# A hybrid decoder step: RWKV's 64-row products alternate between the two halves of the partitions

## The chip, the core and the metric

The kernel runs on one core of a Trainium2 chip. The core has a matrix engine (TensorE, PE in the rows; its weight loads are PEld), VectorE (DVE), ScalarE (ACT), GpSimd (POOL) and SyncE (SP), which work on their own queues, each in order, and wait for each other by semaphores. [...] The metric is the device time of one execution in microseconds (us), the median of the runs.

## The reference

One layer of a decoder for two groups of requests that share weights: a prompt of 2048 tokens, and 8 samples of 8 tokens with caches. A token has 1024 values.

```
sh1, sc1, gt1, sh2, sc2, gt2 = ada_modulation(c)
proj = (rms_norm(x) * (1 + sc1) + sh1) @ w_in          # 1024 -> 1536 (attention) + 1792 (RWKV)
att  = three dilated windows (128,1) (512,4) (2048,16), combined by their log-sums
Pm   = P + (P_prev - P) * mu                            # RWKV: token shift
w    = -softplus(-(w0 + tanh(wl) @ w2)) - 0.5           # low rank, 64 -> 512
a    = sigmoid(a0 + al @ a2)                            # low rank, 64 -> 512
S_t  = S * decay + (S @ -kk) (kk*a)^T + v k^T ;  o = S r # 8 heads of 64 x 64, token by token
x    = x + gt1 * (concat(att, rwkv_output(o)) @ w_out)
x    = x + gt2 * (relu(h2 @ w_ff1)^2 @ w_ff2)           # 1024 -> 4096 -> 1024
```

All inputs and outputs are float32.

## The kernel before, in words

**Tiling and stages.** The prompt is cut into four windows of 512 tokens. A table (ORDER) names the stages and the times at which they are planned: i0 to i3 (norm and input projection), r0 to r3 (RWKV), a0 to a3 (attention), s (the samples' RWKV and attention), and m, p, f (mixing, output projection, MLP). A stage gets a priority that rises with its planned time, and the framework's planner then puts every engine's instructions into one fixed order: it walks through a model of the machine and takes, engine by engine, the ready instruction that comes first by priority. So the large products of the i, p and f stages (PSUM tiles named mmps, written in `mm3`, lines 320 to 322, three products per block since a float32 is split into two parts) stand between the small steps of r, a and s.

**RWKV in groups.** A window of RWKV is four groups of 128 tokens, 16 groups in all, and the samples are one more of 64. A group is two chunks of 64 tokens. Channels lie on partitions: the tile `[128, 4, W]` holds 8 heads of 64 channels as 4 pairs (hp), the even head of a pair on partitions 0 to 63, the odd one on 64 to 127 (par 0 and 1). A product over one head contracts over 64 partitions, so it uses one half of the rows of TensorE's array.

**Three such families are touched.**

- lps, in `rw_elem` (lines 553 to 563): the low-rank products. `wa2` has w2 on partitions 0 to 63 and a2 on 64 to 127; the input is `sg` (named sgl in the rows) for the first and `lm` for the second. Four products for one, into a PSUM tile of one bank, and an addition by VectorE (xx, line 563); then four for the other and its addition.
- btps, in `rw_mats` (lines 639 to 645): bk is transposed, 2 chunks x 4 pairs for par 0 into one bank, copied out by ScalarE (bkT, line 645), then the same for par 1.
- aps, in `rw_mats` (lines 653 to 663): for each chunk, after four transpositions of the values (vtps, line 649, copied to UV by ScalarE, line 650), four products bk x F for par 1 into one bank, three masked copies by VectorE (AT, AT, F; lines 660, 661, 663), then the same for par 0.

**Banks.** These tiles have the tag "e", for which there are two banks; vtps, ssps and bops take the same two, and part of attention's and the samples' tiles too. A tile gets a bank when one is free in the planner's walk.

**What follows.** AT goes through DRAM to `rw_solve` (triangular inverses), then `rw_chunk` carries the state through the two chunks, and `rw_out` normalizes and gates. The next group's `rw_elem` is issued ahead of the chunks of this one.

Of the kernel before, what the change touches and what calls it, by code (L numbers as in the profile page):

```python
# [9 lines left out]
F32 = mybir.dt.float32  # L10
F32R = mybir.dt.float32r
BF16 = mybir.dt.bfloat16
AF = mybir.ActivationFunctionType
# [109 lines left out]
class Step:  # L123
# [407 lines left out]
    def rw_elem(self, V, psv, g):  # L531
        nc = self.nc
        S = g < 0
        W, seg, nch = (64, 8, 1) if S else (128, 64, 2)
# [10 lines left out]
        lm = V.tile([128, 2, W], F32, name="lm", tag="lm")  # L545
        self.rw_mix(V, g, 12, 2, "rawl", lm)
        sg = V.tile([128, 2, W], F32, name="sgl", tag="sgl")
# [2 lines left out]
        nc.vector.tensor_scalar(sg[0:64, 0], sg[0:64, 0], 2.0, -1.0, op0=ALU.mult, op1=ALU.add)  # L550
        r["gl"] = sg[:, 1]
        xx = V.tile([128, 2, 4, W], F32, name="xx", tag="xx")
        for i, (lo, src, bias) in enumerate(((0, sg, self.w0), (64, lm, self.a0))):
            pt = psv.tile([128, 4, W], F32, name="lps", tag="e")
            for hp in range(4):
                nc.tensor.matmul(
                    pt[:, hp],
                    self.wa2[lo:lo + 64, hp * 128:(hp + 1) * 128],
                    src[lo:lo + 64, 0],
                    start=True,  # L560
                    stop=True,
                )
            nc.vector.tensor_tensor(xx[:, i], pt, bias[:, :, None].to_broadcast([128, 4, W]), op=ALU.add)
        xt = V.tile([128, 2, 4, W], F32, name="xt2", tag="xx")
        f4 = lambda t: t.rearrange("p a h t -> p (a h t)")
# [14 lines left out]
        pt = psv.tile([128, 4, W], F32, name="ssps", tag="e")  # L580
# [18 lines left out]
        F = V.tile([128, 4, nch, 128], F32, name="F", tag="F")  # L599
        bk = V.tile([128, 4, nch, 128], F32, name="bk", tag="bk")  # L600
# [29 lines left out]
    def rw_mats(self, V, psv, r, nch, masks):  # L630
        nc = self.nc
        F, bk = r["F"], r["bk"]
        F1 = V.tile([128, 4, nch, 128], F32, name="F1", tag="F1")
        nc.sync.dma_start(F1[0:64], F[64:128])
        UV = V.tile([128, nch, 8, 64], F32, name="UV", tag="UV") if "UV" not in r else r["UV"]
        r["UV"] = UV
        bkT = V.tile([128, nch, 8, 64], F32, name="bkT", tag="bkT")
        AT = V.tile([128, nch * 8, 64], F32, name="AT", tag="AT")
        for par in range(2):
            o = 64 * par  # L640
            pt = psv.tile([128, nch, 4, 64], F32, name="btps", tag="e")
            for c in range(nch):
                for hp in range(4):
                    nc.tensor.transpose(pt[:, c, hp], bk[o:o + 64, hp, c], self.ident[o:o + 64, o:o + 64])
            nc.scalar.activation(bkT[:, :, 4 * par:4 * par + 4], pt, AF.Copy)
        for c in range(nch):
            pt = psv.tile([128, 4, 128], F32, name="vtps", tag="e")
            for hp in range(4):
                nc.tensor.transpose(pt[0:64, hp], r["mv"][:, hp, 64 * c:64 * c + 64], self.ident)
            nc.scalar.activation(  # L650
                UV[64:128, c].rearrange("p h e -> p (h e)"), pt[0:64].rearrange("p h e -> p (h e)"), AF.Copy
            )
            for par in (1, 0):
                o = 64 * par
                pt = psv.tile([128, 4, 128], F32, name="aps", tag="e")
                for hp in range(4):
                    nc.tensor.matmul(pt[:, hp], bk[o:o + 64, hp, c], F[o:o + 64, hp, c], start=True, stop=True)  # L657
                u = (c * 2 + par) * 4
                mb = lambda lo, a, n: masks[lo:lo + 64, None, a:a + n].to_broadcast([64, 4, n])
                nc.vector.tensor_tensor(AT[64:128, u:u + 4], pt[0:64, :, 0:64], mb(0, 0, 64), op=ALU.mult)  # L660
                nc.vector.tensor_tensor(AT[0:64, u:u + 4], pt[0:64, :, 64:128], mb(0, 64, 64), op=ALU.mult)
                dst = (F1 if par else F)[64:128, :, c]
                nc.vector.tensor_tensor(dst, pt[64:128], mb(64, 0, 128), op=ALU.mult)
        r.update(F1=F1, bkT=bkT, AT=AT, AO=AT[0:64])
        if BO == 0:
            self.rw_bonus(V, psv, r)
# [14 lines left out]
    def rw_solve(self, V, psv, r, nch):  # L681

        nc = self.nc
        AT = r["AT"]
        nu = nch * 8
# [3 lines left out]
        for b in range(2):  # L689
            for h in range(2):  # L690
                o = 32 * b + 16 * h
                nc.sync.dma_start(dA[:, b, h].rearrange("u s t -> s u t"), AT[64 + o:80 + o, :, o:o + 16])
        dT = self.dr.tile([nu, 2, 2, 16, 16], F32, name="dT", tag="dT", bufs=3)
# [29 lines left out]
        for b in range(2):  # L723
            lo, hi, o = 64 + 32 * b, 80 + 32 * b, 32 * b
            nc.sync.dma_start(AT[hi:hi + 16, :, o + 16:o + 32], dT[:, b, 1].rearrange("u j i -> j u i"))
            nc.sync.dma_start(AT[lo:hi, :, o:o + 16], dT[:, b, 0].rearrange("u j i -> j u i"))
# [971 lines left out]
```

## Time and profile before

| | |
|---|---|
| median of 3 runs | 3586.67 us (3585.26 to 3594.71) |
| profiled execution | 3593.78 us, its span 3591.7 us |
| TensorE busy | 3317.7 us, 92% of the span, 26546 matmul records |
| weight loads | 2800.1 us, 78% |
| VectorE, ScalarE, GpSimd | 62%, 48%, 29% |

The span is the time from the first to the last instruction of the profiled execution. Busy times come from that one execution. TensorE's products overlap: one starts while the one before still drains, so the distance between starts, not the duration, says what a product costs. [...]

### The profile page before, as it was taken

To read this page: it belongs to the slowest core of one execution; us is meant where nothing else is said; L and a number is where in the kernel's file an instruction comes from. 1 tells how busy PE (TensorE), PEld (TensorE's weight loads), DVE (VectorE), ACT (ScalarE), POOL (GpSimd) and SP (SyncE) were. 2 spreads that over 40 slices of the span, in tenths; PEclk is the share of its full clock that TensorE was granted. 3 is DMA by queue.
4 is the path that set the end of the run, shared out by engine and by line. 5 is a ranking of instruction groups with operands and counts; after the bars stand their busy time and mean duration, and the time that the engine had idled before them with its cause. 6 is when DMAs were issued, how large, how long until landed. Compare 5 with 4: busy or idle time off the path is not lost. (4 is left out here: it accounts for less than half of the span.)

```text
span 3591.7 us, 67893 instructions
## 1 busy us (share of the span) xinstructions
PE 3317.7 (92%) x26546; PEld 2800.1 (78%) x26546; DVE 2241.2 (62%) x4821; ACT 1711.8 (48%) x3156; POOL 1055.9 (29%) x775
## 2 busy tenths in 40 slices
PE   6999999888979999999899999898999999789998
PEld 4886888877968777778877776686777778789998
DVE  3465555635777566778756555454666778655665
ACT  4444353545455555445555432354555445453453
POOL 2322232212233212224321122132112223354464
PEclk7999999989989999899999999999999999899999
DMA  6446644435344542325454234996542325365464
GB/s 231 141 140 172 201 133 134 124 83 101 87 131 131 130 114 83 83 80 169 138 150 124 81 84 131 262 275 212 139 118 87 89 76 166 95 193 153 148 187 153
DMA packets 731769, 496.64 MB, mean 138 GB/s; under 512 B 126134, under 2 KB 682344, under 8 KB 731448
## 3 DMA queue, kind: packets, MB, share of 16 engines
q1 hardware_dynamic: 718824, 479.65, 46.4%
q0 software_dynamic: 12624, 12.65, 1.4%
q8 instruction: 209, 3.42, 0.4%
q14 instruction: 112, 0.92, 0.1%
HBM read 424.11 MB, written 63.77 MB: 136 GB/s over the span
## 5 line engine op out<-in xcount | busy, mean ns | idle before, releaser
L262 POOL TENSOR_TENSOR wl<-stg,wh 128x640 fp32r<-128x640 f32 (+1 forms) x384 | 686.8, 1790 | 1437.7 <-ACT wh L258 1189.7
L258 ACT ACTIVATE wh<-stg 128x1024 fp32r<-128x1024 f32 x384 | 406.2, 1058 | 621.3 <-PE mmps L321 377.7
L320 PE MATMUL mmps<-h2hi,wh 128*128 128x256 f32 (+2 forms) x1864 | 625.0, 336 | 7.9 <-ACT h2hi L306 4.4
L322 PE MATMUL mmps<-h2hi,wl 128*128 128x256 f32 (+2 forms) x1864 | 625.1, 336 | 7.3 <-POOL wl L262 6.9
L321 PE MATMUL mmps<-h2lo,wh 128*128 128x256 f32 (+2 forms) x1864 | 624.8, 335 | 2.9 <-POOL h2lo L308 2.9
L262 DVE TENSOR_TENSOR wl<-stg,wh 128x384 fp32r<-128x384 f32 (+1 forms) x384 | 305.9, 798 | 295.5 <-ACT wh L258 277.8
L321 PE MATMUL mmps<-hid,wh 128*128 128x512 f32 (+2 forms) x1280 | 464.6, 363 | 9.0 <-DVE hid L1429 9.0
L320 PE MATMUL mmps<-hid,wh 128*128 128x512 f32 (+2 forms) x1280 | 465.0, 364 | 2.3 <-ACT wh L258 1.6
L322 PE MATMUL mmps<-hid,wl 128*128 128x512 f32 (+2 forms) x1280 | 464.5, 364 | 1.0 <-POOL wl L262 1.0
L320 PEld LDWEIGHTS mmps<-h2hi,wh 128*128 128x128 f32 x1864 | 357.2, 192 | 38.9 <-ACT h2hi L306 5.3
L322 PEld LDWEIGHTS mmps<-h2hi,wl 128*128 128x128 f32 x1864 | 356.9, 192 | 37.0 <-POOL wl L262 9.5
L321 PEld LDWEIGHTS mmps<-h2lo,wh 128*128 128x128 f32 x1864 | 357.3, 192 | 30.1 <-POOL h2lo L308 3.8
L262 POOL TENSOR_TENSOR wlo<-stg,whi 128x640 fp32r<-128x640 f32 x104 | 182.4, 1768 | 499.5 <-ACT whi L258 461.1
L321 PEld LDWEIGHTS mmps<-hid,wh 128*128 128x128 f32 x1280 | 245.5, 192 | 41.2 <-DVE hid L1429 11.9
L322 PEld LDWEIGHTS mmps<-hid,wl 128*128 128x128 f32 x1280 | 245.8, 192 | 35.0 <-issue 5.8
L320 PEld LDWEIGHTS mmps<-hid,wh 128*128 128x128 f32 x1280 | 245.9, 192 | 33.4 <-ACT wh L258 1.8
L1307 DVE SCALAR_TENSOR_TENSOR acc<-mmps,ada,acc 128x512 f32<-128x512 f32 (+1 forms) x280 | 179.1, 640 | 139.4 <-PE mmps L322 138.2
L320 PE MATMUL mmps<-hhi,whi 128*128 128x512 f32 (+2 forms) x608 | 218.8, 362 | 19.0 <-ACT pev L398 12.3
L320 PE MATMUL mmps<-whi,hhi 128*128 128x256 f32 (+1 forms) x816 | 234.2, 287 | 1.6 <-ACT qev L428 1.6
L321 PE MATMUL mmps<-wlo,hhi 128*128 128x256 f32 (+1 forms) x816 | 234.1, 287 | 0.0
L322 PE MATMUL mmps<-whi,hlo 128*128 128x256 f32 (+1 forms) x816 | 234.0, 287 | 0.0
L321 PE MATMUL mmps<-hlo,whi 128*128 128x512 f32 (+2 forms) x608 | 219.3, 361 | 6.6 <-POOL hlo L308 6.6
(350 smaller groups left out, 6525.9 us busy)
## 6 DMA issues: line engine op xcount, KB each, us to landing
stg<-in_w_ff_dram SPq DMA_DIRECT2D x320, 512.0 KB, 4.2
stg<-in_w_in_dram SPq DMA_DIRECT2D x104, 512.0 KB, 4.7
stg<-in_w_out_dram SPq DMA_DIRECT2D x64, 512.0 KB, 4.6
kst<-in_cache_k_dram SPq DMA_DIRECT2D x80, 256.0 KB, 5.5
vst<-in_cache_v_dram SPq DMA_DIRECT2D x80, 256.0 KB, 5.3
xt<-in_x_prompt_dram SPq DMA_DIRECT2D x32, 512.0 KB, 4.3
wada<-in_w_ada_dram SPq DMA_DIRECT2D x32, 512.0 KB, 3.7
Pd<-pev SPq DMA_DIRECT2D x56, 256.0 KB, 2.8
```

The source lines that it names most:

```text
L258: nc.scalar.activation(hi, src, AF.Copy)
L262: eng.tensor_tensor(lo[:, k], src[:, k], hi[:, k].bitcast(F32), op=ALU.subtract)
L320: nc.tensor.matmul(out, wh(k), xh(k), start=k == 0, stop=False)
L321: nc.tensor.matmul(out, wh(k), xl(k), start=False, stop=False)
L322: nc.tensor.matmul(out, wl(k), xh(k), start=False, stop=k == nk - 1)
L1307: nc.vector.scalar_tensor_tensor(o, pt[:, 0:np_], gt[:, ob, 0:1], o, op0=ALU.mult, op1=ALU.add)
```

## The change

In all three families the two halves' tiles are now made together, and the products alternate between them, one of the lower and one of the upper half of the partitions; the readers (additions, copies, masks) follow after both. For aps the pair starts with par 1 as before, and the reading order is par 1, then par 0.

```diff
-        for i, (lo, src, bias) in enumerate(((0, sg, self.w0), (64, lm, self.a0))):
-            pt = psv.tile([128, 4, W], F32, name="lps", tag="e")
-            for hp in range(4):
+        pts = [psv.tile([128, 4, W], F32, name="lps", tag="e") for _ in range(2)]
+        for hp in range(4):
+            for lo, src, pt in ((0, sg, pts[0]), (64, lm, pts[1])):
                 nc.tensor.matmul(
                     pt[:, hp],
                     self.wa2[lo:lo + 64, hp * 128:(hp + 1) * 128],
...
+        for i, (pt, bias) in enumerate(zip(pts, (self.w0, self.a0))):
             nc.vector.tensor_tensor(xx[:, i], pt, bias[:, :, None].to_broadcast([128, 4, W]), op=ALU.add)
...
+        pts = [psv.tile([128, nch, 4, 64], F32, name="btps", tag="e") for _ in range(2)]
+        for c in range(nch):
+            for hp in range(4):
+                for par in range(2):
+                    o = 64 * par
+                    nc.tensor.transpose(pts[par][:, c, hp], bk[o:o + 64, hp, c], self.ident[o:o + 64, o:o + 64])
         for par in range(2):
-            o = 64 * par
-            pt = psv.tile([128, nch, 4, 64], F32, name="btps", tag="e")
-            for c in range(nch):
-                for hp in range(4):
-                    nc.tensor.transpose(pt[:, c, hp], bk[o:o + 64, hp, c], self.ident[o:o + 64, o:o + 64])
-            nc.scalar.activation(bkT[:, :, 4 * par:4 * par + 4], pt, AF.Copy)
+            nc.scalar.activation(bkT[:, :, 4 * par:4 * par + 4], pts[par], AF.Copy)
...
+            pts = [psv.tile([128, 4, 128], F32, name="aps", tag="e") for _ in range(2)]
+            for hp in range(4):
+                for par in (1, 0):
+                    o = 64 * par
+                    nc.tensor.matmul(pts[par][:, hp], bk[o:o + 64, hp, c], F[o:o + 64, hp, c], start=True, stop=True)
             for par in (1, 0):
-                o = 64 * par
-                pt = psv.tile([128, 4, 128], F32, name="aps", tag="e")
-                for hp in range(4):
-                    nc.tensor.matmul(pt[:, hp], bk[o:o + 64, hp, c], F[o:o + 64, hp, c], start=True, stop=True)
+                pt = pts[par]
```

The planner then orders anew. On TensorE, in the first group's `rw_elem` (lps is the low-rank tile, sgl and lm the two inputs, mmps a block of the projection), the piece of the difference is:

```order
 L321 MATMUL mmps<-hlo,whi 128x512
 L322 MATMUL mmps<-hhi,wlo 128x512
-L556 MATMUL lps<-sgl,wa_1682 128x128 x4
-L556 MATMUL lps<-lm,wa_1682 128x128 x4
+L556 MATMUL lps<-sgl,wa_1682 128x128
+L556 MATMUL lps<-lm,wa_1682 128x128
+L556 MATMUL lps<-sgl,wa_1682 128x128
+L556 MATMUL lps<-lm,wa_1682 128x128
+L556 MATMUL lps<-sgl,wa_1682 128x128
+L556 MATMUL lps<-lm,wa_1682 128x128
+L556 MATMUL lps<-sgl,wa_1682 128x128
+L556 MATMUL lps<-lm,wa_1682 128x128
```

Four and four have become one and one, at the same place among the projection's blocks. All 16 groups of the prompt look so, and their transpositions (btps) too.

On TensorE, in the first group's second chunk, with the tiles' numbers (aps_1882 is par 1 and aps_1890 par 0, vtps the values' transpositions), before:

```order
L649 MATMUL vtps_1876<-ident_90,mv_1809 64x128 x4
L321 MATMUL mmps_1027<-wlo_1015,hhi_249 128x256
L322 MATMUL mmps_1027<-whi_1016,hlo_250 128x256
L320 MATMUL mmps_1027<-whi_1016,hhi_249 128x256
L321 MATMUL mmps_1027<-wlo_1015,hhi_249 128x256
L322 MATMUL mmps_1027<-whi_1016,hlo_250 128x256
L320 MATMUL mmps_1092<-whi_1016,hhi_249 128x256
L321 MATMUL mmps_1092<-wlo_1015,hhi_249 128x256
L657 MATMUL aps_1882<-F_1787,bk_1788 128x128 x4
L657 MATMUL aps_1890<-F_1787,bk_1788 128x128 x4
```

The same place now (aps_1883 is par 1, aps_1882 par 0):

```order
L651 MATMUL vtps_1876<-ident_90,mv_1809 64x128 x4
L321 MATMUL mmps_1027<-wlo_1015,hhi_249 128x256
L322 MATMUL mmps_1027<-whi_1016,hlo_250 128x256
L320 MATMUL mmps_1027<-whi_1016,hhi_249 128x256
L321 MATMUL mmps_1027<-wlo_1015,hhi_249 128x256
L322 MATMUL mmps_1027<-whi_1016,hlo_250 128x256
L320 MATMUL mmps_1092<-whi_1016,hhi_249 128x256
L321 MATMUL mmps_1092<-wlo_1015,hhi_249 128x256
L659 MATMUL aps_1883<-F_1787,bk_1788 128x128 x3
L659 MATMUL aps_1882<-F_1787,bk_1788 128x128 x3
L659 MATMUL aps_1883<-F_1787,bk_1788 128x128
L659 MATMUL aps_1882<-F_1787,bk_1788 128x128
```

Three, three, one and one stand where four and four stood: the second bank was ready in the planner's walk only when three of par 1 were placed. In most chunks the two halves of aps still stand apart, four of one and, after a stretch of mmps, four of the other.

## Rows read from the trace of the kernel before

**Rows 1.** The page's first part: busy us, share of the span, instructions.

```profile
PE 3317.7 (92%) x26546; PEld 2800.1 (78%) x26546; DVE 2241.2 (62%) x4821; ACT 1711.8 (48%) x3156; POOL 1055.9 (29%) x775
```

**Rows 2.** Busy time by stretch, last RWKV window; the columns stand ahead.

```profile
core 0: us, PE busy (x) PEld busy (x) DVE busy (x) ACT busy (x) POOL busy (x), PEclk, DMA share, GB/s
...
2756.00:3060.00 304.00, 289.24 (x2338) 231.15 (x2338) 245.54 (x470) 156.52 (x290) 91.99 (x87) 0.99 0.38 109
```

**Rows 3.** TensorE's groups by line: shapes, count, busy us, mean ns, idle before, releasers.

```profile
L657 PE MATMUL aps<-F,bk 64*128 64x128 f32 x528 | 83.3, 302 | 1.2 <-ACT UV L650 1.1
...
L556 PE MATMUL lps<-sgl,wa 64*128 64x128 f32 (+1 forms) x136 | 21.2, 301 | 11.3 <-DVE sgl L550 10.5 <-DVE sol L714 0.7
...
L644 PE MATMUL btps<-ident,bk 64*128 64x64 f32 x264 | 18.9, 237 | 8.0 <-DVE bk L620 6.6 <-DVE bk L619 1.4
```

**Rows 4.** Timeline, TensorE, first lps block: start us, us, instruction, count.

```profile
128.85 0.82 PE L556 MATMUL lps<-sgl,wa 64*128 64x128 f32 x5
129.40 0.37 PE L556 MATMUL lps<-lm,wa 64*128 64x128 f32 x1
129.51 0.27 PE L556 MATMUL lps<-sgl,wa 64*128 64x128 f32 x1
129.62 0.27 PE L556 MATMUL lps<-lm,wa 64*128 64x128 f32 x1
129.62 0.27 PE L556 MATMUL lps<-sgl,wa 64*128 64x128 f32 x1
129.73 0.27 PE L556 MATMUL lps<-lm,wa 64*128 64x128 f32 x1
129.73 0.27 PE L556 MATMUL lps<-sgl,wa 64*128 64x128 f32 x1
129.84 0.72 PE L556 MATMUL lps<-lm,wa 64*128 64x128 f32 x5
130.49 0.50 PE L320 MATMUL mmps<-hhi,whi 128*128 128x512 f32 x1
```

**Rows 5.** Timeline, TensorE: aps runs of one, four, and four and four.

```profile
242.50 0.49 PE L657 MATMUL aps<-F,bk 64*128 64x128 f32 x2
242.91 0.64 PE L225 MATMUL mps<-wada,cT 128*32 128x256 f32 x8
...
865.63 1.16 PE L657 MATMUL aps<-F,bk 64*128 64x128 f32 x8
866.72 0.38 PE L320 MATMUL mmps<-hhi,whi 128*128 128x256 f32 x1
...
377.97 1.71 PE L657 MATMUL aps<-F,bk 64*128 64x128 f32 x16
379.61 0.38 PE L322 MATMUL mmps<-whi,hlo 128*128 128x256 f32 x1
```

**Rows 6.** Timeline, TensorE: a whole btps block, and a broken one.

```profile
153.26 0.98 PE L644 MATMUL btps<-ident,bk 64*128 64x64 f32 x16
154.18 0.39 PE L322 MATMUL mmps<-whi,hlo 128*128 128x256 f32 x1
...
3016.44 0.71 PE L644 MATMUL btps<-ident,bk 64*128 64x64 f32 x9
3017.08 0.33 PE L1477 MATMUL trps<-ident,acc 128*128 128x128 f32 x1
```

**Rows 7.** TensorE's waits: waiting line, releaser, us in total, times, longest us.

```profile
PE lps L556 <- DVE sgl L550: 10.5, 5, 5.6
...
PE btps L644 <- DVE bk L620: 6.6, 4, 3.4
...
PE btps L644 <- DVE bk L619: 1.4, 2, 1.1
...
PE aps L657 <- ACT UV L650: 1.1, 1, 1.1
```

**Rows 8.** The copies out of btps: count, least, median and most ns.

```profile
L645 ACT ACTIVATE bkT<-btps x34: 365/593/599, 154.9 to 3021.6; 128x512 f32<-128x512 f32 x32, 128x256 f32<-128x256 f32 x2
```

## The prediction

> **What bounds the kernel now.** I read the page's busy shares first, then the stretches of the RWKV windows, then the three groups of products that the change touches, their rows in order of time, and last what they wait for. TensorE is busy 92% of the span, no other engine is near that [rows 1], and in the last RWKV window (2756 to 3060 us) it is busy 289 of 304 us at a granted clock of 0.99 [rows 2]. Its queue is in order, and the planner lays the projection's and the MLP's products (mmps) between the steps of RWKV. So I first ask how much TensorE time the change takes out, and then how much of that the rest can follow.
>
> The touched groups are 528 records for the matrices (aps), 136 for each half of the low rank (lps) and 264 for the transpositions (btps) [rows 3]. An fp32 product leaves two records, a transposition one: 33 chunks x 8 products x 2 = 528, 17 groups x 4 x 2 = 136, 16 x 16 + 8 = 264.
>
> **How two halves run already.** [Rows 4] is a whole lps block. Five records of sgl (partitions 0 to 63) start 0.11 us apart; at 129.40 the first of lm (64 to 127) starts although three of sgl are still to come; then one of each starts at 129.62, and again at 129.73, each half keeping its 0.11 us. So halves with banks of their own do run side by side at full pace, and the order of before already uses this where they meet, for about 3 of 8 records. The block takes 128.85 to 130.49, 1.64 us. The price of a single half is in [rows 5]: four aps products (8 records), 865.63 to 866.72, 1.09 us; one alone, 242.50 to 242.91, 0.41 us, so about 0.41 + 0.23 (n-1) us for n products: some 0.2 us of a run is spent once, whatever its length. Four and four of the same chunk in a row take 377.97 to 379.61, 1.64 us, as in lps.
>
> **Part by part.** No instruction is added or removed; on each engine the same ones stand in another order.
>
> lps: in the new order 16 of 17 blocks alternate product by product. If both halves keep the pace of [rows 4], a block costs what one half costs, 1.09 us: 16 x (1.64 - 1.09) = 8.8 us. The sample's block keeps four, filler, four.
>
> btps: 16 blocks alternate. Before, a block takes 153.26 to 154.18, 0.92 us; nine transpositions, eight of them of one half, take 3016.44 to 3017.08, 0.64 us [rows 6]. 16 x 0.28 = 4.5 us.
>
> aps: here the order does only part of what the code says. The two banks are seldom free at the same moment (one has held vtps, the other the last btps or aps), and the planner takes what is ready. Counted in the order: before, 29 runs of one product, 9 of two, 13 of three and 25 of four, all of one half, 7 of four and four, and 4 shorter mixed ones (an estimated 4.6 us in all from the same pitches). At 0.41, 0.64, 0.86, 1.09 and 1.64 us that is 11.9 + 5.8 + 11.2 + 27.3 + 11.5 + 4.6 = 72.3 us. Now 19, 14, 6 and 22 one-sided runs, 4 of four and four, 4 of the form three, three, one, one (estimated 1.3 us: half the overlap), and 9 that alternate wholly or nearly so, which I price at their longer half, 7.5 us: 7.8 + 9.0 + 5.2 + 24.0 + 6.6 + 5.2 + 7.5 = 65.3 us. It gives 7.0 us, half of it from fewer and longer runs, not from alternating. If the planner's order gave nothing, 0; if all 33 chunks alternated, 33 x 1.09 = 36 us would be left, but the order shows that they don't.
>
> Sum on TensorE: 8.8 + 4.5 + 7.0 = 20.3 us.
>
> What it does not shorten is RWKV's own chain. The first half of a block ends no sooner than before, and its readers still come one after the other: two copies of bkT of 0.593 us each [rows 8] finish about when they did, because the second had to wait for ScalarE's first and not for TensorE. The same holds for the two additions after lps and the masks after aps. So the time comes back only where TensorE would otherwise go on at once with filler and the next RWKV step is ready when it comes sooner. TensorE stood waiting at lps for sgl 5 times, at btps for bk 4 + 2 times, out of 17 blocks each [rows 7]: at about a third of the blocks the chain is late already, and there what was saved before them becomes a longer wait. I take two thirds: 20.3 x 2/3 = 13.5 us. The bounds of this share are 0 and 1.
>
> The profiled execution is 3593.8 us (3591.7 of span and 2.1 around it), 7.1 above the median of the runs, 3586.7. From its own time the sum gives 3580.3, from the median **3573.2 us**.
>
> The added wait: both banks must be free before the second product of a pair. Behind it in TensorE's queue stands whatever the planner put there, mostly mmps. Nothing of before prices it exactly: aps waited for the copy out of vtps (UV) once, 1.1 us [rows 7], the lower bound is 0 since the planner puts filler ahead of the second bank (last pair of order rows), and the upper bound a copy of 0.593 us at each of 17 + 17 + 33 = 67 places, 40 us. I take 0, nearest to the one wait seen, and keep the other end as a rival.
>
> **The rivals.**
> Not passed on (the filler is done sooner, then TensorE waits for VectorE and ScalarE): for it, the unshortened chain; against it, 289 of 304 us busy. Gain 0 to 6.8 us, a share under a third: about 3583 us.
>
> More than forecast: halves that did not overlap before, as if the pairs of starts in [rows 4] were only drawn so. Then the blocks of 1.64 and 0.92 us hold 16 records one behind the other, alternating takes half of each, and 16 x 0.82 + 16 x 0.46 + 7.0 = 27.5 us come free, two thirds of it 18 us: 3568 us. Against it: eight records of one half take 1.09 us by themselves and cost 0.11 us more each, so 16 in strict order would be 1.09 + 8 x 0.11 = 1.97 us and not the 1.64 of the rows. [...]
>
> Slower: the second bank. If the bank is still held on the chip by a reader that the planner thought done, TensorE stands still with the filler behind it. At 0.593 us for all 67 places the loss is 40 us, net of 13.5 about 26 us: 3613 us. It decides from 13.5 / 67 = 0.20 us per place. For it: the planner's costs are not the chip's, and a pair needs two free banks where one did. Against it: such waits are nearly absent before.
>
> The alternation that doesn't happen: true for most aps already by the order and in the sum; without any aps gain 13.3 x 2/3 = 8.9 us, 3577.8, inside the forecast's own range.
>
> **How the numbers follow.** A difference under 0.3% (10.8 us: 3575.9 to 3597.4) can't be told from none here. Forecast 0.60, with shares of one third to one: 3566 to 3580 us, two thirds of it below 3575.9. Not passed on 0.20, nearly all of it no change. No overlap before 0.08, faster. Second bank 0.12, slower. Faster: 0.39 + 0.08 = 0.47. Same: 0.21 + 0.18 = 0.39. Slower: 0.12 + 0.02 = 0.14. The range for 8 in 10 reaches from the full 27.5 us, 3559, to the upper part of no change, 3596, where some moved filler or a few waits for a bank still fit.
>
> **What would show it.** Right: lps blocks of about 1.1 us with sgl and lm starting in pairs, btps blocks of about 0.64 us, aps runs of 1.09 us still one-sided in most chunks, and TensorE's idle time at lps, btps and ssps up by 5 to 10 us. Wrong: blocks that stay at 1.6 us (two halves don't run together product by product), TensorE waits of half a microsecond at lps or aps for xx, bkT or UV (the second bank), or a granted clock in the last window below the 0.99 of [rows 2] because TensorE stands still more often.

## The result, and the profile after

| | before | after |
|---|---|---|
| median (7 runs each) | 3586.67 us (3582.4 to 3594.71) | 3608.16 us (3600.33 to 3616.86) |
| profiled execution, span | 3593.78, 3591.7 us | 3615.23, 3613.5 us |
| mean granted clock | 0.964 | 0.959 |
| TensorE busy, idle within the span | 3317.7, 274.1 us | 3323.0, 290.5 us |
| time at half clock | 259.9 us | 295.0 us |

The changed kernel is slower: ratio 1.0054, 95% interval 1.0036 to 1.0072. The forecast was 3573.2 us, 0.4% faster, and the time lies above the range. TensorE's idle time is the span less the busy time; the granted clock (PEclk) is, as the profile gives it, a share of full speed. In slices of 0.2 us both traces show 1.0 or 0.5, and a mean between them only where a slice holds a step from one to the other; the time at half clock is the sum of the stretches at 0.5.

The page's first part after, against [rows 1]:

```profile
PE 3323.0 (92%) x26546; PEld 2797.6 (77%) x26546; DVE 2240.5 (62%) x4821; ACT 1712.5 (47%) x3156; POOL 1055.1 (29%) x775
```

TensorE is busier by 5.3 us and idler by 16.4 us, although the blocks became shorter. That they did, the first lps block shows, against [rows 4] (timeline of TensorE; start us, us, instruction):

```profile
125.38 0.40 PE L322 MATMUL mmps<-hhi,wlo 128*128 128x512 f32 x1
125.71 0.37 PE L556 MATMUL lps<-sgl,wa 64*128 64x128 f32 x1
125.72 0.37 PE L556 MATMUL lps<-lm,wa 64*128 64x128 f32 x1
125.92 0.27 PE L556 MATMUL lps<-sgl,wa 64*128 64x128 f32 x1
125.93 0.27 PE L556 MATMUL lps<-lm,wa 64*128 64x128 f32 x1
126.03 0.27 PE L556 MATMUL lps<-sgl,wa 64*128 64x128 f32 x1
126.04 0.27 PE L556 MATMUL lps<-lm,wa 64*128 64x128 f32 x1
...
126.59 0.27 PE L556 MATMUL lps<-sgl,wa 64*128 64x128 f32 x1
126.60 0.27 PE L556 MATMUL lps<-lm,wa 64*128 64x128 f32 x1
126.80 0.50 PE L320 MATMUL mmps<-hhi,whi 128*128 128x512 f32 x1
```

From its second record on each half keeps its 0.11 us from record to record (the first step is 0.21), and the other half starts 0.01 us behind it: 125.71 to 126.80, 1.09 us, where it was 1.64. The first btps block, against [rows 6]:

```profile
150.04 0.71 PE L645 MATMUL btps<-ident,bk 64*128 64x64 f32 x16
150.68 0.39 PE L322 MATMUL mmps<-whi,hlo 128*128 128x256 f32 x1
```

0.64 us, where it was 0.92. These two are no exceptions: of the prompt's 16 lps blocks the 14 that run at full clock take 1.09 us each, and the 11 btps blocks that run unbroken at full clock take 0.64 or 0.65. So the pairs do on TensorE what was forecast. What undoes it stands in the busy times by stretch (columns as in [rows 2]), after:

```profile
815.00:960.00 145.00, 121.99 (x1111) 112.59 (x1111) 87.68 (x258) 61.41 (x126) 29.51 (x31) 0.87 0.46 100
2756.00:3060.00 304.00, 294.31 (x2268) 230.72 (x2266) 237.88 (x467) 152.80 (x283) 89.35 (x88) 0.94 0.36 101
3012.00:3051.00 39.00, 37.23 (x358) 29.11 (x358) 18.27 (x31) 11.79 (x23) 5.02 (x7) 0.56 0.26 79
```

The same stretches before, beside [rows 2]:

```profile
815.00:960.00 145.00, 126.45 (x1220) 118.33 (x1219) 95.79 (x297) 66.30 (x134) 30.40 (x32) 0.95 0.47 103
3012.00:3051.00 39.00, 37.41 (x515) 32.45 (x516) 31.36 (x52) 18.74 (x42) 11.17 (x10) 1.00 0.62 199
```

Read the third number from the end first, the granted clock. At the end of the last RWKV window it is 0.56 instead of 1.00, although TensorE is as busy, 37 of 39 us. At the start of the second window it is 0.87 instead of 0.95. The counts of records must not be compared in such a window, because at the same time after the start two runs stand at different work. A second trace of the kernel before (a run described below) has as few records there at full clock:

```profile
3012.00:3051.00 39.00, 37.00 (x352) 32.49 (x348) 32.51 (x52) 18.58 (x40) 15.25 (x13) 1.00 0.57 178
```

So the two kernels are set side by side at the same mmps record; both have 13704 of them, which are counted through. The stretches are chosen so that TensorE has the same records in them, up to four. From record 3250 to 4500, the start of the second window, after takes 14.2 us longer, with 27.3 us more at half clock. From 10050 to 10700, the last RWKV group and what follows, it takes 16.9 us longer, with 44.4 us more at half clock. The rest of the kernel gives back 9.3 us of these 31.1, since the spans differ by 21.8. These two places are the loss. Against the second trace of the kernel before they are 10.5 and 15.1 us; outside them the two traces of that one kernel differ by up to 8 us in a stretch.

The one lps block of after that runs at half clock with no wait behind it takes 2.01 us where the others take 1.09, not quite twice as long. So time at half clock costs at most half of itself, by estimate 13.7 and 22.2 us at the two places. 14.2 and 16.9 us were lost, so the clock can account for nearly all of it.

How each begins, after:

```profile
857.19 0.27 PE L651 MATMUL vtps<-ident,mv 128*64 128x128 f32 x1 [1.71 <-DVE mv L520]
...
859.54 1.22 PE L659 MATMUL aps<-F,bk 64*128 64x128 f32 x4 [1.35 <-ACT bkT L647]
860.68 0.42 PE L651 MATMUL vtps<-ident,mv 128*64 128x128 f32 x1
861.03 0.79 PE L659 MATMUL aps<-F,bk 64*128 64x128 f32 x2
...
3013.74 0.39 PE L322 MATMUL mmps<-hid,wl 128*128 128x512 f32 x1
3015.90 0.98 PE L738 MATMUL yps<-sol,AT 16*16 16x16 f32 x64 [1.77 <-DVE sol L726]
3016.81 0.79 PE L320 MATMUL mmps<-hid,wh 128*128 128x512 f32 x1
3017.41 0.41 PE L1481 MATMUL trps<-ident,acc 128*128 128x128 f32 x1
3017.47 0.78 PE L321 MATMUL mmps<-hid,wh 128*128 128x512 f32 x1
```

At the first place TensorE waits 1.71 us for VectorE's mv and 1.35 us for ScalarE's copy out of btps, at the second 1.77 us for VectorE's sol. Then two products of aps (four records) take 1.14 us, where the forecast had 0.64 for two, and the mmps record behind yps lasts 0.79 us, where before it lasts 0.50. From 3017 on the clock is at half for 34.1 us. The same step before found sol ready and kept the full clock:

```profile
3012.49 0.33 PE L1477 MATMUL trps<-ident,acc 128*128 128x128 f32 x1 [1.21 <-DVE acc L1307]
...
3013.13 0.40 PE L322 MATMUL mmps<-hid,wl 128*128 128x512 f32 x1
3013.45 0.97 PE L734 MATMUL yps<-sol,AT 16*16 16x16 f32 x64
3014.35 0.50 PE L320 MATMUL mmps<-hid,wh 128*128 128x512 f32 x1
```

TensorE's waits after (waiting line, releaser, us in total, times, longest), against [rows 7]:

```profile
PE lps L556 <- DVE sgl L550: 9.6, 4, 6.0
PE vtps L651 <- DVE mv L520: 7.7, 6, 1.9
PE yps L738 <- DVE sol L726: 5.5, 5, 3.1
...
PE ssps L528 <- DVE xx L564: 3.1, 2, 2.6
PE btps L645 <- DVE bk L621: 3.1, 3, 2.6
PE btps L645 <- DVE sol L712: 3.0, 1, 3.0
PE aps L659 <- ACT bkT L647: 1.9, 3, 1.4
```

Before, vtps waited for mv 4.5 us in 4 places and yps for sol 2.1 us in 3.

### The profile page after: what moved, and what is told of

Same layout as the page of the kernel before. It is cut to its first block, busy times and chain, and to the rows that moved or that the text cites. A ratio compares the mean times of both kernels' runs of the same rounds, so it can differ in the third digit from the quotient of the medians.

```text
span 3613.5 us, 67916 instructions
## 1 busy us (share of the span) xinstructions
PE 3323.0 (92%) x26546; PEld 2797.6 (77%) x26546; DVE 2240.5 (62%) x4821; ACT 1712.5 (47%) x3156; POOL 1055.1 (29%) x775
## 5 line engine op out<-in xcount | busy, mean ns | idle before, releaser
L320 PE MATMUL mmps<-h2hi,wh 128*128 128x256 f32 (+2 forms) x1864 | 630.7, 339 | 10.5 <-ACT h2hi L306 4.4
L262 DVE TENSOR_TENSOR wl<-stg,wh 128x384 fp32r<-128x384 f32 (+1 forms) x384 | 314.6, 821 | 287.9 <-ACT wh L258 275.1
L322 PEld LDWEIGHTS mmps<-h2hi,wl 128*128 128x128 f32 x1864 | 360.8, 194 | 38.1 <-POOL wl L262 11.4
```

The lines of the kernel that those rows point to most:

```text
L262: eng.tensor_tensor(lo[:, k], src[:, k], hi[:, k].bitcast(F32), op=ALU.subtract)
L320: nc.tensor.matmul(out, wh(k), xh(k), start=k == 0, stop=False)
L322: nc.tensor.matmul(out, wl(k), xh(k), start=False, stop=k == nk - 1)
```

## The experiments

Theory one (theory order below): the loss is the planner's new order of everything, by way of the granted clock; the pairs themselves cost nothing. Rivals: the pairs themselves cost, by a wait for the second bank (theory bank) or by a fall of the clock (theory clock). Beside it stands the question why TensorE's saving is not a gain. The experiments ran on three chips, each with the kernel before beside them. Its medians there were 3596.93 us (first four experiments), 3602.29 (next four) and 3593.09 (last two), so ratios are compared, not times. A ratio comes with its 95% interval.

**The pairs without the new order.** Kernel before, planned as before; then on TensorE the 41 blocks (16 lps, 15 btps, 10 aps) where one half follows the other directly are zipped in place.

```diff
+                one = [L[k] for k, t in zip(at, tiles) if t == tiles[0]]
+                two = [L[k] for k, t in zip(at, tiles) if t != tiles[0]]
+                new = _zip(one, two)
...
+    return [i for p in zip(one, two) for i in p] + one[m:] + two[m:]
```

> Every instruction of every engine stands in the order of the kernel before; only inside the 41 blocks in which two halves already stood one behind the other on TensorE (16 lps, 15 btps, 10 aps) do the products now alternate. Theory order (the pairs give back TensorE time, the loss comes from the planner's new order of everything else): lps 16 x 0.55 + btps about 14 x 0.27 + aps about 8 x 0.5 = 16 us of TensorE time, two thirds passed on, about 3576 us, faster than before. Theory clock (the pairs themselves make TensorE run dry and the granted clock fall, wherever they stand): 3595 to 3612 us, as the changed kernel. Theory bank (a pair waits for its second bank with the queue behind it): slower than before, with waits at lps or aps for the readers of the bank.

Measured: 3603.97 us, ratio 1.0016 (0.9999 to 1.0034): neither the gain that theory order expected nor the whole loss. Its page (first part; before: [rows 1]):

```profile
PE 3309.7 (92%) x26546; PEld 2790.5 (78%) x26546; DVE 2236.2 (62%) x4821; ACT 1711.5 (48%) x3156; POOL 1054.1 (29%) x775
```

Busy 8.0 us less, span 3599.6 us, so idle 289.9, 15.8 more: what was taken out of TensorE stands there as waiting, and the time is no better. (The second trace of the kernel before has 281.8 us idle, against which it is 8.1 more.) About half of it has a place, the first product behind the low rank's block (ssps). Its waits, kernel before:

```profile
PE ssps L529 <- DVE sql L526: 7.3, 8, 2.7
PE ssps L528 <- ACT sqh L525: 5.5, 2, 5.2
PE ssps L528 <- DVE xx L563: 0.8, 2, 0.5
```

and with the pairs in place:

```profile
PE ssps L528 <- ACT sqh L525: 8.6, 5, 6.2
PE ssps L529 <- DVE sql L526: 8.6, 7, 2.7
PE ssps L528 <- DVE xx L563: 3.9, 7, 1.1
```

13.6 us became 21.1: 7.5 us, against 16 x 0.55 = 8.8 us saved at lps (5.3 us against the 15.8 of the second trace of before). The products got to the end of the filler sooner, and what ssps needs from VectorE and ScalarE was not ready sooner.

Waiting is not all. The clock fell here too: the mean granted clock of the 12 runs is 0.962, that of the 31 runs of the kernel before beside them 0.966. In the profiled execution it fell at the second place:

```profile
3012.00:3051.00 39.00, 38.14 (x342) 33.30 (x341) 24.20 (x41) 15.56 (x35) 9.13 (x9) 0.75 0.48 157
```

From record 10050 to 10700, in the same order as before, this kernel takes 13.2 us longer, with 34.1 us more at half clock. So pairs can cost clock without any new order, as theory clock said, and theory one is too simple where it says that the pairs cost nothing. The second bank isn't it: aps waits 2.7 us for UV and bkT together, where it was 1.1.

**The new order without the pairs.** Kernel after; on TensorE its 48 paired blocks are put back to half after half, with the same code but for one line.

```diff
+                new = one + two
```

> The changed kernel's order on every engine, but inside each of 48 blocks on TensorE the products of one half stand ahead of the other's again. Theory order: slower than the changed kernel by what the pairs gave, 3608 + 10 to 16 = 3618 to 3624 us. Theory clock or theory bank: the loss goes with the pairs, 3582 to 3592 us, as the kernel before.

Measured: 3627.09 us, ratio 1.0061 (1.0038 to 1.0084), clock 0.956 in the profiled execution. As slow as after, with no pair left. At the two places it takes 22.5 us (47.8 more at half clock) and 15.6 us (41.0) longer than before. The new order without any pair loses as much as the change. The 10 to 16 us that the missing pairs were expected to add don't show in the ratio, though its interval doesn't exclude them.

**Another order without any pair.** Kernel before, with the planned times of the i, p, f and m stages later by one unit:

```diff
-GL = 250
+GL = 249
```

> The kernel before with one number of the plan changed (projection and MLP stages planned 249 instead of 250 us ahead), so that the planner sets some hundred instructions elsewhere, with no pair anywhere; the last RWKV group stands nearly where the changed kernel has it. Theory order: a move of either sign of up to 20 us, and slower (3595 to 3610 us) if the place of the last RWKV group is what costs. Theory clock or bank: nothing of the pairs is in it, 3580 to 3593 us.

Measured: 3609.23 us, ratio 1.0027 (1.0008 to 1.0045). An order that differs only by this costs half as much as the change. Its profiled execution was the quickest of its 12 (3594.29 us): in it 10.9 us are lost at records 3250 to 4500, with 27.3 us more at half clock, and won back elsewhere; the second place loses 3.1 us. So in this trace the place of the last RWKV group, the reason expected for a slower time, cost next to nothing. What the median lost, the quickest run can't show, and the clock alone isn't it: its mean over the runs is 0.965, against 0.966 for the kernel before.

**Two families in a new order.** Kernel after with aps as before (one half's four products, its readers, then the other's).

```diff
-            pts = [psv.tile([128, 4, 128], F32, name="aps", tag="e") for _ in range(2)]
...
+                pt = psv.tile([128, 4, 128], F32, name="aps", tag="e")
```

> lps and btps alternate, aps is written as before; planned anew. Theory order: within 15 us of the changed kernel or of the kernel before according to where the planner puts the steps around 850 us and 3015 us; TensorE's lps blocks are 1.09 us and btps blocks 0.64 us in either case. Theory bank at aps: the loss is gone, 3570 to 3580 us. Theory clock: slower than before, 3595 to 3608 us.

Measured: 3606.89 us, ratio 1.0021 (1.0007 to 1.0036); 18.7 us are lost at the first place, with 34.1 us more at half clock, and none at the second (0.4 us less than before). The loss at the first place doesn't need aps in pairs.

**The new order, its clock held.** Kernel after; ahead of 7 waits at the two places the first product of the mmps block before is repeated, 80 repeats in all, into the bank that it is about to write, so that TensorE works where it would wait.

```diff
+HOLD = {3432: 14, 3483: 10, 3489: 8, 3672: 24, 3829: 10, 10239: 7, 10361: 7}
```

Each entry is the number of an mmps record and the repeats at the start of the block ahead of it.

> The changed kernel in its own order, with 80 products more on TensorE: just ahead of seven waits of 1.35 to 4.3 us after which the granted clock falls in the changed kernel's trace (842 to 921 us, and 3014 and 3073 us), the first product of the nearest mmps block is repeated 7 to 24 times, which leaves the results as they are. About 12 us of work. Theory clock (the half clock after waits in the two stretches costs the 22 us): fewer us at half clock there, and 8 to 25 us faster than the changed kernel in spite of the added work. Theory chain (the waits are RWKV's chain and the clock is a side effect that costs nothing): the same time as the changed kernel. Theory bank: 0 to 12 us slower than the changed kernel.

Beside it the kernel after once more:

> The changed kernel once more, beside the two above on the same chip, for its ratio and for a second trace. If the place of the half clock is fixed by the order, the stretches at 820 to 950 us and 3015 to 3050 us are at half clock again (44 to 65 us and 20 to 34 us); if it is chance, they lie elsewhere and the time moves with them. Ratio to before 1.002 to 1.007.

and one execution of the kernel before:

> The kernel before once more, for a second trace. If the half clock is fixed by the order, 255 to 265 us of it again, 38 us of them between 815 and 1100 us and none between 2990 and 3050 us; if it moves from run to run, 245 to 300 us, and the time with it by about half of the difference.

Measured: with the repeats 3604.29 us, ratio 1.0007 (0.9987 to 1.0027); after 3622.4 us, 1.0058 (1.0033 to 1.0082); before, that one run, 3587.08 us, against a median of 3602.29 beside it. That run was 229.8 us at half clock, where 245 to 300 had been expected and the first trace had 259.9: of the kernel before itself the half clock moves by 30 us, though both traces have the full clock from 3012 to 3051 us. After shows its loss again at both places (19.2 and 12.7 us against the first trace of before, with 37.5 and 30.7 us more at half clock). With the repeats, by stretch:

```profile
815.00:960.00 145.00, 129.90 (x1247) 121.52 (x1248) 92.72 (x279) 62.47 (x125) 30.61 (x32) 0.93 0.42 96
3012.00:3051.00 39.00, 38.50 (x515) 31.91 (x514) 30.79 (x50) 18.04 (x36) 8.62 (x9) 1.00 0.47 140
```

0.87 went up to 0.93 and 0.56 to 1.00. Counted from record to record, with the repeats as extra work, the two places take 10.6 and 9.5 us less than in the second trace of after, each with 23.9 us less at half clock. Work was added and the kernel became faster by 18 us, and the two intervals don't overlap: what these waits cost is for the most part not their own length but the clock behind them.

**Pairs in place, clock held.** The first experiment's kernel, with 344 repeats ahead of 29 waits. Each of these had a fall of the clock shortly behind it, in the trace of this kernel or in that of the kernel before.

```diff
+HOLD = {513: 14, 960: 7, 1095: 8, 1203: 5, 1922: 16, 2449: 16, 2928: 21, 3036: 24, 3102: 21, 3228: 14, 3312: 11, 3336: 24, 3337: 9, 3432: 15, 5022: 9, 5345: 8, 5654: 10, 5697: 3, 6602: 9, 8120: 12, 8168: 6, 8818: 9, 8888: 19, 9558: 13, 9625: 10, 10242: 3, 10440: 7, 10759: 13, 11184: 8}
```

> The order of before with the 41 blocks alternating in place, and 344 repeated first products (about 55 us of work) ahead of 29 waits that both the kernel before and the in-place kernel show, each after which the clock falls within 5 us in one of the two traces. Theory clock: the half clock goes down from about 260 us by 80 us or more, and the time by up to 40 us, 3550 to 3585 us. Theory chain: the repeats fill waits and change nothing, 3595 to 3605 us. If the repeats don't fit into the waits: up to 3640 us.

Measured: 3582.22 us, ratio 0.9949 (0.9932 to 0.9966), faster than the kernel before and the kernel after beside it. The mean granted clock is 0.974 against 0.964 of the kernel before.

**What of that the pairs give.** The same repeats at the same 29 places in the kernel before, and the kernel with pairs and repeats again beside it.

> The kernel before, with no pair alternated, and the same 344 repeated products ahead of the same 29 waits as in hold_in_place. Clock alone: the gain of hold_in_place over the kernel before came from the clock, and the pairs give nothing even when the clock is held: ratio 0.993 to 0.997 to the kernel before, within 0.2% of hold_in_place, with a granted clock of 0.97 or more. Pairs and clock: the pairs' saved time is only worth something while the clock is held: ratio 0.998 to 1.003, hold_in_place 0.3 to 0.7% ahead of it.

> hold_in_place once more, on the chip of hold_before: ratio 0.993 to 0.997 to the kernel before. If it comes out at 1.000 or above, the first run's gain was that chip's.

Measured: 3582.22 us, ratio 0.9974 (0.9952 to 0.9996), without pairs, and 3583.29 us, 0.9976 (0.9958 to 0.9994), with them. The repeats alone give the gain; the pairs give none that can be seen, even with the clock held (each ratio is known to about 0.2%, so some 8 us either way are open; the kernel with pairs gave 0.9949 on one chip and 0.9976 on another). Here the clock is no rival: its mean over the runs is 0.974 with pairs and 0.975 without. Two profiled executions at nearly the same clock, of the kernel with pairs in its first experiment and of the one without, have 0.973 and 0.972 (spans 3586.2, 3591.0 us). Without pairs, then with:

```profile
PE 3356.6 (93%) x26890; PEld 2841.1 (79%) x26890; DVE 2237.2 (62%) x4821; ACT 1711.8 (48%) x3156; POOL 1062.1 (30%) x775
...
PE 3345.2 (93%) x26890; PEld 2824.6 (79%) x26890; DVE 2238.4 (62%) x4821; ACT 1712.1 (48%) x3156; POOL 1058.5 (30%) x775
```

Busy 11.4 us less, idle 234.4 and 241.0, 6.6 us more: 4.8 us reach the span, and ssps again takes most of the rest (13.1 us of waits for sql, sqh and xx without pairs, 18.4 with them).

The repeats did not hold the clock everywhere. From record 10050 to 10700 the kernel before with repeats, which has neither a pair nor a new order, takes 209.5 us with 58.0 at half clock, against 193.7 and 23.9 without them. What it gains, it gains elsewhere. All traces over the same records (time in us, then how much of it at half clock; the rows with the clock held count their repeats in):

| | 3250 to 4500 | 10050 to 10700 |
|---|---|---|
| before, two traces | 277.3, 37.5; 280.9, 51.2 | 193.7, 23.9; 195.5, 30.7 |
| after, two traces | 291.4, 64.9; 296.5, 75.1 | 210.6, 68.3; 206.4, 54.6 |
| pairs in place | 278.9, 47.8 | 206.9, 58.0 |
| halves, new order | 299.8, 85.3 | 209.3, 64.9 |
| GL 249 | 288.2, 64.9 | 196.8, 30.7 |
| lps and btps in pairs | 296.0, 71.7 | 193.3, 34.1 |
| new order, clock held | 285.9, 51.2 | 196.9, 30.7 |
| before, clock held | 275.3, 30.7 | 209.5, 58.0 |
| in place, clock held, two traces | 281.2, 47.8; 275.1, 37.5 | 209.2, 54.6; 208.9, 54.6 |

The loss at the first place goes with a new order; it stands in no trace with the old one. The loss at the second place goes with more time at half clock in every row, but the old order has it too.

## Why the prediction was wrong

- **What bounds the kernel.** TensorE's share and its full queue were read rightly; but 289 of 304 us busy does not say that it is busy at full clock next time. The stretch that was the witness, 0.99 in [rows 2], has 0.94 after.
- **lps, btps.** Right, to the hundredth: 1.09 and 0.64 us a block. The rival that halves did not overlap before falls with it, since alternating would then have made them 0.82 and 0.46.
- **aps, and the sum of 20.3 us.** Not settled to its size. At nearly equal clock 11.4 us of busy time are gone with 41 blocks in place, where about 16 were expected. In after the saving can't be read off the busy time alone, since it has 35 us more at half clock.
- **Two thirds passed on.** This step failed. The chain of RWKV was named as not shortened, but the share was taken from how many blocks of these families waited already. The wait moved on to the next product that needs the chain, which the count did not include. In place no time was won: idle rose by 15.8 us (8.1 against the second trace of before) and the clock fell from 0.966 to 0.962. With the clock held nothing came through by the ratios, and 4.8 of 11.4 us between two profiles. The sign that TensorE's idle time at lps, btps and ssps would grow by 5 to 10 us came true in place, at ssps. In after the three together stand at 31.9 us against 32.8 before, and the new waits are at vtps and yps. A wait that is expected to grow should be a term of the sum, not only a sign.
- **What the sum left out, and what decided the sign.** This step failed too, and it made a loss out of no gain. The change was priced as blocks, but it also makes the planner order everything anew. That order had no term, neither for its new waits (vtps for mv, yps for sol) nor for the clock behind them. Halves in the new order lose as much as the change (ratio 1.0061 against 1.0054), pairs in the old order less (1.0016, not clear of none), and 80 repeated products take the loss away (1.0007). The granted clock stood in the prediction as a sign of being wrong, which came true (0.94 in the window of [rows 2]), with no price and no rival of its own.
- **The second bank.** Nearly absent, as taken: aps waits for bkT 1.9 us in 3 places. One of these, 1.35 us at 859.54, stands right ahead of a half-clock stretch, so it may have helped to set that one off; but the new order without pairs loses as much at that place. The rival's 3613 us is near the time measured, for another reason.

What stays open: why just these waits let the clock fall and others of the same length do not, what part each of the seven has, and what lets it fall at the second place in the old order, with pairs or with repeats elsewhere, when two traces of the kernel before keep it. An order can't be judged by its waits alone, since the kernel before waits 1.21 us at 3012.49 for acc, in the same stage, and keeps 1.00.

## What to carry to other kernels

Shorter blocks on the busiest engine are worth something only where the next step's inputs are ready sooner (with the pairs in place, 8.0 us less busy stood beside 15.8 us more idle); look for the first product behind the block that waits for another engine, and put the saving there as a wait before putting it into the sum. Where a planner orders anew, run the new order without the edit and the edit without the new order: here the first lost as much as the change, and the second gained nothing. Compare two traces from the same instruction to the same instruction, not over the same microseconds, and take a second trace of the unchanged kernel before naming a place. And where a low granted clock follows a wait, repeating a large product ahead of that wait can be worth more than the edit (0.2 to 0.5% here).

## What had not been expected of the hardware

- The granted clock stayed at half while TensorE was busy: after, 37.23 of 39.00 us at 0.56 from 3012 to 3051 us, and from 3017 on all of 34.00 us at 0.50. About two thirds of the products there use 16, 32 or 64 rows (186 of 269 records). The kernel before has 1.00 over the same 39 us, with 37.41 and 37.00 us busy in its two traces, so busy time, as the profile counts it, doesn't tell the two apart.
- Waits of 1.35 to 1.77 us stand right ahead of half-clock stretches, at two places that cost 14.2 and 16.9 us.
- The time at half clock moves between runs of one kernel: 259.9 and 229.8 us in the two traces of the kernel before, whose 31 runs beside the first experiments range from a clock of 0.959 to 0.972. Two profiles of the kernel after differ by 10.8 us of span at clocks of 0.959 and 0.956.
- An order that differs by one planned unit (GL 249) moves the time by 0.27%, about half of what the whole change did.
